# Two pads in on-chip memory that move the weight slots of a two-layer decoder trunk from 288 to 96 bytes past a multiple of 512

## The chip, the core and the metric

The kernel runs on one core of one Trainium2 chip. The metric is the device time of one execution in microseconds (us), and the median of several executions is quoted. Five engines work side by side: TensorE (PE; its weight loads are shown as PEld), VectorE (DVE), ScalarE (ACT), GpSimd (POOL) and SyncE (SP), whose queue issues nearly all transfers. SBUF, the on-chip memory, has 128 partitions; a tile of shape [128, n] in 4-byte numbers takes 4n bytes at the same place in every partition. "Place" below means that byte offset in the partition, modulo 512.

## The reference

It computes two layers of a conditioned decoder trunk for 256 tokens with 1024 features, in 32-bit floats, and a last RMSNorm. Each layer has three sub-layers, whose shift, scale and gate come from `mod = silu(c) @ w_ada[l] + b_ada[l]`:

```python
x = x + 0.5 * g1 * swiglu(modulate(x, sh1, sc1), ffn1_gate, ffn1_up, ffn1_down)
x = x + g2 * token_mix(modulate(x, sh2, sc2), ...)
x = x + 0.5 * g3 * swiglu(modulate(x, sh3, sc3), ffn2_gate, ffn2_up, ffn2_down)
```

`swiglu(u)` is `(silu(u @ w_gate) * (u @ w_up)) @ w_down` with 2816 hidden features. `token_mix` projects `u` with one matrix, runs two attention branches, gates them and multiplies with `w_out`.

## The kernel before

**Exact products from split operands.** A weight is read from memory in pieces of 1 MB into one of four `raw` slots. `split_unit` (lines 147 to 175) cuts a piece into units of 1024 columns: ACT copies a rounded part to `whi` (line 169) and DVE writes the remainder to `wlo` (line 174). Activations are split the same way (`uhi`/`ulo`, `hh`/`hl`, `oa`, `ob`, `yt`, `yk`). Each product is three matmuls, hi by hi, hi by lo and lo by hi. All matmuls are issued by the helper `mm`, so their line is 103; transposes have line 106.

**Two forms of product.** In `ws_tile` the weight part is the stationary operand (128 by 128) and the activations of 256 tokens stream past it: 24 matmuls of 256 columns for a unit. In `xs_group` the activations are stationary and the weight part streams: 12 matmuls of 512 columns for a unit. Names in the trace are out<-moving,stationary: `mm<-uhi,whi` is the first form, `mm<-whi,hh` the second.

**Where the parts of a weight lie.** There are four ordinary slots for a unit, in the pool `wsp` (four `whi`, four `wlo`). During a feed-forward sub-layer the pool `fu` has three more. Units take them in turn, four from `wsp` and then three from `fu`, by `unit_kinds[:] = ["w"] * 4 + ["f"] * EXTRA`, beginning anew with each such sub-layer. The mixer uses `wsp` and, for some units, tiles that are free at the time (`ux`, `uq`, `us` and others). One feed-forward sub-layer has 66 units: 8 of the second form for the first 512 hidden features, 36 of the first form for the other nine groups of gate and up, and 22 of the second form for the down product. The very first sub-layer has 12, 32 and 22, since `begin` makes the first 768 hidden features in another order. A mixer has 8 units of the first form in `wsp` with `uhi`/`ulo` streaming, and 10 units of the second form in `wsp` against `oa`, `ob` and `yt`.

**Places.** The pools are laid out in the order in which the code opens them: `const`, `raws`, `wsp`, `keep`, `scr`, `small`, and then, for one sub-layer at a time, `ffn` with `fu`, or `tm`. The sizes of their tiles give these places modulo 512:

| Tiles | Place before |
|---|---|
| the four `raw` slots | 288 |
| the four ordinary `whi` and `wlo` slots (`wsp`) | 288 |
| `x`, `uhi`, `ulo` and all of `keep` and `scr` | 288 |
| `hh`, `hl`, `oa`, `ob`, `yt`, `ux`, `uq`, `us`, the first sub-layer's `room` (`ffn`, `tm`) | 96 |
| the three further `whi` and `wlo` slots (`fu`) | 96 |
| `yk` (`tm`) | 192 |

A stationary block of a unit of the first form is 512 bytes long, and the next one begins where it ends; `uhi` and `ulo` advance by 1024 bytes; a streaming row of 512 columns is 2048 bytes. So within a unit the place of each operand stays what the table says.

**Order.** SP's queue issues the weights' transfers in order, each when the `raw` slot is released by DVE (or ACT). Splits run in order on ACT and DVE, with the work on adaLN vectors (`ada_half`, line 217) between them. Between sub-layers, `norm_mod` needs the whole residual sum and its square sum, so that PE has little to do for a short time; this is called a handover below. The first sub-layer's `begin` has its own order, with weights landing in the `room` tiles, which lie where `hh` and `hl` will be.

Of the kernel before, what the change touches and what calls it, by code (L numbers as in the profile page):

```python
# [10 lines left out]
F32 = mybir.dt.float32  # L11
# [5 lines left out]
P = 128  # L17
# [17 lines left out]
def shape_tables():  # L35
    f = np.float32
    tab = np.zeros((P, TAB_END), f)
    r = np.arange(P)[:, None]
    k = np.arange(S)[None, :]
    dist = (P + r - k).astype(f)  # L40
    vis = k <= P + r
    tab[:, TAB_D:TAB_D + S] = np.where(vis, dist, f(NEG))
    tab[:, TAB_M:TAB_M + S] = np.where(vis, f(0), f(NEG))
    slopes = np.array(SLOPES, f)
    cend = 16 * np.arange(16) + 31
    c = np.zeros((P, NH, H, 16), f)
    for hf in range(NH):
        t = hf * P + np.arange(P)
        ok = (cend[None, :] <= t[:, None]) & (np.arange(16) < 15)[None, :]
        dd = (t[:, None] - cend[None, :]).astype(f)  # L50
        c[:, hf] = np.where(ok, dd, f(NEG))[:, None, :]
    tab[:, TAB_C:TAB_C + NH * H * 16] = c.reshape(P, -1)
    half = 16
    inv = (10000.0 ** (-np.arange(half, dtype=np.float64) / half)).astype(f)
    ang = (np.arange(S, dtype=f)[:, None] * inv[None, :]).astype(f)
    cos, sin = np.cos(ang.astype(np.float64)).astype(f), np.sin(ang.astype(np.float64)).astype(f)
    sc = f(-(96.0 ** -0.5))
    tt = np.full((P, S), sc, f)
    tt[64:80] = tt[80:96] = cos.T * sc
    tt[96:112] = -sin.T * sc  # L60
    tt[112:128] = sin.T * sc
    tab[:, TAB_T:TAB_T + S] = tt
    cs = np.concatenate([cos, cos], 1).reshape(NH, P, 32).transpose(1, 0, 2)
    sn = np.concatenate([-sin, sin], 1).reshape(NH, P, 32).transpose(1, 0, 2)
    tab[:, TAB_COS:TAB_COS + 64] = cs.reshape(P, 64)
    tab[:, TAB_SIN:TAB_SIN + 64] = sn.reshape(P, 64)
    hh = np.arange(P)[:, None] // 16
    tab[:, TAB_BD:TAB_BD + H] = np.where(hh == np.arange(H)[None, :], f(0.5), f(0))
    tab[:, TAB_SL:TAB_SL + H] = slopes[None, :]
    # slopes are powers of two: queries carry -1 / (8 slope) exactly  # L70
    tab[:64, TAB_Q:TAB_Q + 4] = f(-0.125) / slopes[None, :4]
    tab[64:, TAB_Q:TAB_Q + 4] = f(-0.125) / slopes[None, 4:]
    tab[:, TAB_COL:TAB_COL + 32] = (np.arange(P)[:, None] % 32 == np.arange(32)[None, :]).astype(f)
    return tab
# [3 lines left out]
def hybrid_trunk(ctx, tc, t, out):  # L78
    nc = tc.nc
# [4 lines left out]
    EXTRA = 3            # pairs of weight parts that the feed-forward phases hold beyond four  # L84
    DELAY = (3, 4)       # units of products before a half's operands are turned
    SPLITS_AHEAD = (0, 6)
    keep = ctx.enter_context(tc.tile_pool(name="keep", bufs=1))
# [32 lines left out]
    nc.scalar.activation(cact, c_in, AF.Silu)  # L120
    x = keep.tile([P, NH, D], F32, name="x")
    colmask = tab[:, TAB_COL:TAB_COL + 32]

# [15 lines left out]
    # a normalisation that the tensor engine will wait for is not to queue behind later splits  # L139
# [3 lines left out]
    def hold(n, dve, act):  # L143
        """the splits from the n-th on queue behind these"""
        holds.append([n, dve.ins, act.ins])
# [32 lines left out]
    # shift and scale as columns [feature % 128, feature // 128]; gates as rows on every partition  # L178
    mods = {}

    def column_sums(ps, vec, a, start, stop):
        """ps[32 i + *, j * 32 + r] += sum over partitions of vec * a[:, j * 128 + 32 i + r]"""
        av = a.rearrange("p (j i r) -> p j i r", j=4, i=4)
        for i in range(4):
            mm(ps[32 * i:32 * i + 32, :P].rearrange("p (j r) -> p j r", j=4), vec, av[:, :, i, :], start, stop)
# [118 lines left out]
    def norm_mod(hf, uhi, ulo, sc, sh):  # L304
        """chain on the vector engines now; returns the rest, with its transposes, to be run later"""
        r, a, sq = half_rstd(hf)
        xn = scr.tile([P, D], F32, name="xn", tag="s4")
        for b in range(2):
            i = nc.vector.tensor_scalar(xn[:, b * 512:(b + 1) * 512], x[:, hf, b * 512:(b + 1) * 512], r, a,
                                        ALU.mult, ALU.mult)  # L310
        hold(SPLITS_AHEAD[hf], i, sq)

        def rest(bs=(0, 1)):
            for b in bs:
                uf = scr.tile([P, 4, P], F32, name="uf", tag="uf", bufs=2)
                ps = trps()
                for i in range(4):
                    tr(ps[:, i * P:(i + 1) * P], xn[:, (b * 4 + i) * P:(b * 4 + i + 1) * P])
                for i in range(4):
                    k = b * 4 + i  # L320
                    if i % 2 == 1:
                        nc.scalar.activation(uf[:, i, :], ps[:, i * P:(i + 1) * P], AF.Identity,
                                             scale=sc[:, k:k + 1], bias=sh[:, k:k + 1])
                    else:
                        nc.vector.tensor_scalar(uf[:, i, :], ps[:, i * P:(i + 1) * P],
                                                sc[:, k:k + 1], sh[:, k:k + 1], ALU.mult, ALU.add)
                o = slice(hf * P, (hf + 1) * P)
                nc.scalar.activation(uhi[:, b * 4:b * 4 + 4, o], uf, AF.Copy)
                nc.vector.tensor_tensor(ulo[:, b * 4:b * 4 + 4, o], uf,  # L329
                                        uhi[:, b * 4:b * 4 + 4, o].bitcast(F32), ALU.subtract)  # L330
        return rest

    # work put off by some units of a product
# [25 lines left out]
    def xs_gemm(units, shi, slo, n, evac, tail, post=None):  # L359
        """out[token half, n] = u^T.T @ W; units: (split on demand, [k...]); the last `tail` units  # L360
        are run for the first half of the tokens, then for the second"""
        xs_group([(units, n, evac, tail)], shi, slo, post)

    def xs_group(gemms, shi, slo, post=None):
        """products with the same stationary operand; all their tails by token half"""
# [34 lines left out]
    def stream_units(wv, nk, n, kper, uper, ada_every=0, kinds=None):  # L400
        """wv: [P, nk, n] DRAM view; raw pieces of kper k-tiles, units of uper."""
# [34 lines left out]
    def ffn(l, which, uhi, ulo, ada_plan, post, xn=None, side=None):  # L436
# [4 lines left out]
        with tc.tile_pool(name="ffn", bufs=1) as fp, tc.tile_pool(name="fu", bufs=EXTRA) as fu, \  # L441
# [10 lines left out]
            # the first four tiles token-major, so that they can begin with half of the tokens  # L452
            gp = []

            def finish_rows(hf, gate, up, f0):
                """the product of both for some tiles, token-major, turned"""
# [20 lines left out]
            def begin():  # L477
                """the first sub-layer's start: its shift and scale come in quarters of the features, each
                followed by these features' products with six tiles of hidden features"""
# [6 lines left out]
                # weights wait where the hidden features will be  # L486
# [141 lines left out]
    def token_mix(l, uhi, ulo, ada_plan, post):  # L628
        uhk, ulk = ktiles(uhi), ktiles(ulo)
        w_in = t["w_in"][l].rearrange("(k p) n -> p k n", p=P)  # L630
        with tc.tile_pool(name="tm", bufs=1) as tp, tc.tile_pool(name="aps", bufs=2, space=PSUM) as aps:
# [7 lines left out]
            # merge gates, token-major: tanh(g/2)  # L639
# [20 lines left out]
            # nsa gates, compressed q and kv of the latent branch, rotary key: token-major  # L660
# [21 lines left out]
            # rstd of cq (scaled sums) and ckv together  # L682
# [4 lines left out]
            # compressed branch: windows of k, v  # L687
# [19 lines left out]
            # selected and window keys, feature-major, split, each key head on both halves of the partitions  # L707
# [41 lines left out]
            # gelu (tanh form), doubled; keys on partitions 0-63, values on 64-127  # L749
# [11 lines left out]
            # values, token-major [tok, khalf, (s, w), (g, dv)]  # L761
# [38 lines left out]
            # values, token-major  # L800
# [10 lines left out]
            # rotary key, twice, on partitions 64-127  # L811
# [21 lines left out]
            def latent_operands(j):  # L833
                """queries and keys of heads 2j, 2j+1 with the rotary parts on partitions 64-127"""
# [30 lines left out]
            # q, feature-major, both parts of a head stacked: with the doubled keys two products are exact  # L865
# [22 lines left out]
            # compressed scores, softmax  # L888
# [35 lines left out]
            def softmax(s, pv, dist, slope, gcol):  # L924
                """s[:, a] <- gate * softmax(-slope * (pv[:, a] + dist)); dist is huge where masked"""
# [259 lines left out]
```

## Time and profile before

| | |
|---|---|
| median of 3 runs | 1209.77 us (1209.32 to 1212.08) |
| profiled execution, first to last instruction | 1209.5 us |
[...]
| PE matmul busy | 1172.7 us, 97% |
| DVE busy | 946.5 us, 78% |
| ACT busy | 641.2 us, 53% |
| 16 DMA engines, queue of the weights | 68.9% of the span |

Busy time of PE is modelled and overlapping, so that the interval from the start of one matmul to the start of the next is a better measure of its pace than the duration of one. The profiled execution's span lies 0.3 us under the median of the runs.

### The profile page before, as it was taken

What the parts mean: (1) busy time and instruction counts of PE and PEld (TensorE: products, weight loads), DVE (VectorE), ACT (ScalarE), POOL (GpSimd) and SP (SyncE); (2) the same over time, 40 slices, a digit from 0 to 9 for tenths busy, and PEclk for the clock granted to TensorE, in tenths of its full rate; (3) what the DMA queues carried; (4) which work ended last, traced back from release to release, by engine and by line L of the source; (5) the groups of instructions that cost most, each with busy time, mean ns of one, the idle gap of its engine ahead of it and who ended that gap; (6) DMA issues with size and microseconds to landing.
All of it is one profiled execution on the core that took longest, in us unless ns stands there. A gap on an engine that the chain in (4) does not pass through costs nothing.

```text
span 1209.5 us, 20210 instructions
## 1 busy us (share of the span) xinstructions
PE 1172.7 (97%) x7886; PEld 1027.3 (85%) x7886; DVE 946.5 (78%) x1885; ACT 641.2 (53%) x1152; POOL 19.1 (2%) x17
## 2 busy tenths in 40 slices
PE   5999999899999999999999999999999999999997
PEld 3799987689867889998879999787997778999985
DVE  4998997878888898798478879955878888865553
ACT  4444544547676564434465445444677756554441
POOL 0000000100000000000000000001000000000000
PEclk9999999999999999999999999998999999999999
DMA  9989999495623578898739989954664254885530
GB/s 328 336 294 321 344 336 337 152 253 174 174 102 108 174 229 287 286 311 311 248 110 312 311 274 360 340 168 137 178 188 115 83 187 128 288 263 197 174 140 35
DMA packets 201970, 274.95 MB, mean 227 GB/s; under 512 B 13613, under 2 KB 119815, under 8 KB 201875
## 3 DMA queue, kind: packets, MB, share of 16 engines
q1 hardware_dynamic: 201119, 273.02, 68.9%
q8 instruction: 62, 1.02, 0.3%
q10 hardware_dynamic: 756, 0.64, 0.2%
q14 instruction: 33, 0.27, 0.1%
HBM read 272.60 MB, written 1.05 MB: 226 GB/s over the span
## 4 chain that ended last, share of the span: by engine, by line
PE 86%; DVE 7%; DMA 3%; issue 2%; ACT 1%; SPq 1%; DVEq 0%; ACTq 0%
PE mm L103 77%; PE tr L106 3%; DVE wlo L174 2%; DMA raw<-in_w_ada 2%; PE sc L103 2%; PE po L103 2%; PE tr L103 2%; ACT whi L169 0%; DVE rs L297 0%; DVE acc L217 0%; DVE x L432 0%; DVE rtmp L431 0%; DMA c_in<-in_c 0%; DVE win L702 0%; DVE acc L520 0%
## 5 line engine op out<-in xcount | busy, mean ns | idle before, releaser
L174 DVE TENSOR_TENSOR wlo<-raw,whi 128x1024 fp32r<-128x1024 f32 (+5 forms) x400 | 427.8, 1084 | 128.4 <-ACT whi L169 127.2
L169 ACT ACTIVATE whi<-raw 128x1024 fp32r<-128x1024 f32 (+5 forms) x400 | 364.1, 936 | 236.9 <-PE mm L103 103.9
L103 PE MATMUL mm<-uhi,whi 128*128 128x256 f32 x1248 | 353.1, 283 | 0.0
L103 PE MATMUL mm<-ulo,whi 128*128 128x256 f32 x1248 | 351.8, 282 | 0.0
L103 PE MATMUL mm<-uhi,wlo 128*128 128x256 f32 x1248 | 351.8, 282 | 0.0
L103 PEld LDWEIGHTS mm<-uhi,whi 128*128 128x128 f32 x1248 | 238.9, 191 | 2.4 <-issue 1.4
L103 PEld LDWEIGHTS mm<-ulo,whi 128*128 128x128 f32 x1248 | 237.5, 190 | 0.5
L103 PEld LDWEIGHTS mm<-uhi,wlo 128*128 128x128 f32 x1248 | 237.4, 190 | 0.0
L217 DVE SCALAR_TENSOR_TENSOR acc<-raw,cact,acc 128x512 f32<-128x512 f32 x224 | 166.9, 747 | 6.0 <-DMA raw<-in_w_ada 3.1
L103 PE MATMUL mm<-whi,hh 128*128 128x512 f32 x352 | 139.5, 396 | 0.0
L103 PE MATMUL mm<-wlo,hh 128*128 128x512 f32 x352 | 138.2, 393 | 0.0
L103 PE MATMUL mm<-whi,hl 128*128 128x512 f32 x352 | 138.2, 393 | 0.0
L103 PE MATMUL mm<-whi,uhi 128*128 128x512 f32 (+3 forms) x336 | 126.9, 380 | 3.9 <-ACT uhi L533 2.6
L103 PE MATMUL mm<-wlo,uhi 128*128 128x512 f32 (+3 forms) x336 | 125.9, 375 | 3.7 <-DVE wlo L174 3.7
L103 PE MATMUL mm<-whi,ulo 128*128 128x512 f32 (+3 forms) x336 | 127.2, 379 | 1.7 <-DVE ulo L329 1.7
L103 PEld LDWEIGHTS mm<-whi,hh 128*128 128x128 f32 x352 | 66.0, 187 | 16.5 <-issue 1.6
L103 PEld LDWEIGHTS mm<-whi,hl 128*128 128x128 f32 x352 | 66.0, 188 | 15.4
L103 PEld LDWEIGHTS mm<-wlo,hh 128*128 128x128 f32 x352 | 66.0, 188 | 14.7
L474 ACT ACTIVATE hh<-hf 128x256 fp32r<-128x256 f32 x70 | 29.2, 417 | 92.1 <-DVE hf L473 91.9
L103 PEld LDWEIGHTS mm<-whi,uhi 128*128 128x128 f32 x336 | 63.5, 190 | 14.8 <-ACT uhi L533 3.4
L103 PEld LDWEIGHTS mm<-wlo,uhi 128*128 128x128 f32 x336 | 64.0, 190 | 14.0 <-DVE wlo L174 4.8
L103 PEld LDWEIGHTS mm<-whi,ulo 128*128 128x128 f32 x336 | 64.0, 191 | 12.5 <-DVE ulo L329 3.5
(241 smaller groups left out, 1344.3 us busy)
## 6 DMA issues: line engine op xcount, KB each, us to landing
raw<-in_w_ada SPq DMA_DIRECT2D x72, 1024.0 KB, 8.8
raw<-in_ffn_gate SPq DMA_DIRECT2D x41, 1024.0 KB, 6.6
raw<-in_ffn_up SPq DMA_DIRECT2D x41, 1024.0 KB, 6.0
raw<-in_ffn_down SPq DMA_DIRECT2D x40, 1024.0 KB, 7.5
raw<-in_w_in SPq DMA_DIRECT2D x18, 1024.0 KB, 5.5
raw<-in_w_in SPq DMA_DIRECT2D x16, 512.0 KB, 6.4
raw<-in_w_out SPq DMA_DIRECT2D x8, 1024.0 KB, 5.3
raw<-in_ffn_down SPq DMA_DIRECT2D x8, 512.0 KB
```

Source lines behind the costliest of these rows:

```text
L103: nc.tensor.matmul(o, a, b, start=start, stop=stop)
L106: nc.tensor.transpose(o, a, ident)
L169: nc.scalar.activation(a, s, AF.Copy)
L174: nc.vector.tensor_tensor(b, s, a.bitcast(F32), ALU.subtract)
L217: nc.vector.scalar_tensor_tensor(acc, rv[:, jj, :], cj, binit if j + jj == 0 else acc, ALU.mult, ALU.add)
L474: nc.scalar.activation(h[0][:, f, :], hf32, AF.Copy)
```

## The change

The new code takes two tiles that nothing reads: 320 bytes in `const`, and 192 bytes in `keep` ahead of `x`. POOL clears each once near the start.

```diff
     cact = const.tile([P, KD], F32, name="cact")
     nc.scalar.activation(cact, c_in, AF.Silu)
+    apart = keep.tile([P, 48], F32, name="apart")
+    nc.gpsimd.memset(apart, 0.0)
     x = keep.tile([P, NH, D], F32, name="x")
     colmask = tab[:, TAB_COL:TAB_COL + 32]

+    def pad(pool, nbytes):
+
+        p = pool.tile([P, nbytes // 4], F32, name="pad", tag="pad%d" % nbytes, bufs=1)
+        nc.gpsimd.memset(p, 0.0)
+    pad(const, 320)
```

The rest of the diff removes comments. By the order of the pools the 320 bytes move `raws` and `wsp` from place 288 to place 96 (288 + 320 = 512 + 96). The 192 bytes make it 512 bytes in all for everything from `x` on, which therefore keeps its place modulo 512: `uhi`, `ulo` stay at 288, `hh`, `hl` and the slots of `fu` at 96. The four `raw` slots move along with the ordinary weight slots, and two small constant tiles that come after the pad (`bcols`, `cols`) move as well.

## Rows read from the trace of the kernel before

**Rows 1.** The page: PE busy; DMA share by 40 slices; the chain by engine.

```profile
PE 1172.7 (97%) x7886; PEld 1027.3 (85%) x7886; DVE 946.5 (78%) x1885; ACT 641.2 (53%) x1152; POOL 19.1 (2%) x17
...
DMA  9989999495623578898739989954664254885530
...
PE 86%; DVE 7%; DMA 3%; issue 2%; ACT 1%; SPq 1%; DVEq 0%; ACTq 0%
```

**Rows 2.** Timeline of PE, 1094 to 1115 us, at unit starts: start us, duration us.

```profile
1094.77 0.28 PE L103 MATMUL mm<-uhi,whi 128*128 128x256 f32 x1
...
1097.65 0.28 PE L103 MATMUL mm<-uhi,whi 128*128 128x256 f32 x1
...
1106.29 0.28 PE L103 MATMUL mm<-uhi,whi 128*128 128x256 f32 x1
...
1109.12 0.28 PE L103 MATMUL mm<-uhi,whi 128*128 128x256 f32 x1
...
1114.77 0.28 PE L103 MATMUL mm<-uhi,whi 128*128 128x256 f32 x1
```

**Rows 3.** Timeline of PE in a down product, 1154 to 1174 us.

```profile
1154.31 0.39 PE L103 MATMUL mm<-whi,hh 128*128 128x512 f32 x1
...
1165.51 0.39 PE L103 MATMUL mm<-whi,hh 128*128 128x512 f32 x1
...
1173.69 0.39 PE L103 MATMUL mm<-whi,hh 128*128 128x512 f32 x1
```

**Rows 4.** Timeline of PE from the first mixer's end into the next sub-layer.

```profile
405.66 1.55 PE L103 MATMUL mm<-ux,yt 128*128 128x512 f32 x6
...
408.42 2.97 PE L103 MATMUL mm<-us,yk 128*128 128x512 f32 x12
411.23 0.40 PE L103 MATMUL mm<-whi,yt 128*128 128x512 f32 x1
...
414.02 0.39 PE L103 MATMUL mm<-whi,yk 128*128 128x512 f32 x1
...
423.33 0.39 PE L103 MATMUL mm<-whi,uhi 128*128 128x512 f32 x1
...
428.80 0.40 PE L103 MATMUL mm<-whi,uhi 128*128 128x512 f32 x1
...
431.09 0.39 PE L103 MATMUL mm<-whi,uhi 128*128 128x512 f32 x1
...
433.83 0.39 PE L103 MATMUL mm<-whi,uhi 128*128 128x512 f32 x1
```

**Rows 5.** Groups by form: DVE's remainder of a unit, by source: busy us, mean ns.

```profile
L174 DVE TENSOR_TENSOR wlo<-raw,whi 128x1024 fp32r<-128x1024 f32 x320 | 391.9, 1234 | 112.4 <-ACT whi L169 111.7
...
L174 DVE TENSOR_TENSOR wlo<-room,whi 128x1024 fp32r<-128x1024 f32 x8 | 9.6, 1220 | 3.7 <-ACT whi L169 3.7
```

**Rows 6.** Waits: who waited for whom, us in total, times, longest us.

```profile
ACT whi L169 <- PE mm L103: 105.9, 94, 3.3
...
PE mm L103 <- DVE wlo L174: 3.7, 2, 1.9
```

**Rows 7.** DMA, 11.5 to 13.5 us, then 44.5 to 46.5 us.

```profile
DMA packets 425, 0.76 MB, mean 378 GB/s; under 512 B 27, under 2 KB 85, under 8 KB 425
...
DMA packets 409, 0.74 MB, mean 368 GB/s; under 512 B 22, under 2 KB 77, under 8 KB 409
```

**Rows 8.** The chain at the handovers after both `ffn1`: start us, us.

```profile
213.45 0.70 DVE rtmp L431
...
234.22 1.84 PE mm L103 x8
...
803.21 0.70 DVE rtmp L431
...
824.83 17.18 PE mm L103 x72
```

**Rows 9.** Windows in the second of them: PE, PEld, DVE, ACT, POOL busy, granted clock, DMA.

```profile
821.00:824.00 3.00, 2.25 (x9) 1.47 (x8) 2.62 (x7) 2.60 (x4) 0.33 (x1) 0.50 0.96 322
824.00:827.00 3.00, 3.00 (x11) 2.52 (x10) 2.73 (x6) 2.30 (x5) 0.00 (x0) 0.59 0.44 134
```

## Prediction

> **What bounds the kernel now.** I read the page first. PE is busy for 97% of the span, and the chain that ended last runs through PE for 86% of it, with DVE at 7% and DMA at 3% [rows 1]. A change of PE's pace is therefore worth its full amount unless the feed of weights cannot follow. The waits say that it mostly can: PE's matmuls waited for a split only twice, 3.7 us in total, while ACT waited 105.9 us for PE to give a weight slot back [rows 6]. In other words, over much of the run the splits are ahead of PE and stand still until PE has used a slot.
>
> The second view is the timeline of PE inside the feed-forward products, and it carries the argument. The change alters no instruction there, only places; so I looked for a place that already shows a different pace. The kernel makes that comparison itself, because its units take four slots at place 288 and then three slots at place 96 in turn, with the same instructions on the same streaming operand.
>
> **Gate and up (first form, 24 matmuls of 256 columns per unit).** From 1094.77 to 1106.29 us lie four units from the ordinary slots, 11.52 us, so 2.880 us each; from there to 1114.77 us lie three units from the further slots, 8.48 us, so 2.827 us each [rows 2]. The streaming operand is at 288 throughout. So a unit costs 0.053 us more, 2.2 ns per matmul, when the weights that are loaded behind it lie at 288 too than when they lie at 96. Inside a unit the weights advance by 512 bytes and the streaming operand by 1024 and the pace does not change, so higher bits of the address can't be what matters; that leaves the place modulo 512, or something about the pools themselves (a rival, below). After the change the ordinary slots are at 96, and I take 2.827 us for them. By the rule of four and three, 21 of the 36 units are ordinary in three sub-layers, and 18 of 32 in the first: 81 units x 0.053 = 4.3 us.
>
> **Down (second form, 12 matmuls of 512 columns per unit).** Here the weight streams and `hh` and `hl`, at 96, are stationary. Four ordinary units take 1165.51 - 1154.31 = 11.20 us, 2.800 each; three further ones take 1173.69 - 1165.51 = 8.18 us, 2.727 each [rows 3]. The difference is 0.073 us, 6 ns per matmul. 13 of the 22 units are ordinary in each of four sub-layers: 52 x 0.073 = 3.8 us.
>
> **The mixers.** Eight units per layer have the first form with `uhi` and `ulo`: 16 x 0.053 = 0.85 us. Ten per layer stream from ordinary slots against operands at 96 (`oa`, `ob`, `yt`). Near 411 us 12 such matmuls take 414.02 - 411.23 = 2.79 us, and 12 that stream from tiles at 96 against the same `yt` take 408.42 - 405.66 = 2.76 us [rows 4]; this is a gain of 0.03, against 0.073 in the down product. Between these ends I take 0.05, since the sample here is short and the down product has the same two places: 20 x 0.05 = 1.0 us, between 0.6 and 1.5. In the mixers PE is not always what ends last; I count three quarters, 1.4 us of 1.85.
>
> **Products that I cost at nothing.** The second form against `uhi`/`ulo`, at 288: 24 matmuls from ordinary slots take 428.80 - 423.33 = 5.47 us, 0.228 us each, and 12 from the further slots 433.83 - 431.09 = 2.74 us, again 0.228 [rows 4]. Place 96 brings nothing there. Against `yk`, at 192, streaming from 96 takes 411.23 - 408.42 = 2.81 us for 12; only two units per layer are touched, so even 0.02 us for each is under 0.1 us. The 192 matmuls of the mixers that stream `cT` (already at 96) past ordinary weights go from a pair (96, 288) to a pair (96, 96), of which I have no undisturbed row; at 2.2 ns either way that is 0.4 us up or down, and I take zero.
>
> **The other things that move.** The splits read a `raw` slot at 288 and write an ordinary slot at 288; both go to 96. DVE's remainder took 1220 ns on average when its source was `room`, at 96, and 1234 ns from `raw` [rows 5], so I see no cost and count no gain. POOL clears two small tiles once; POOL is busy 2% [rows 1], its clears come after the one that the start needs, and nothing reads the result. Cost nothing; were the start to wait for them, it would be a fraction of a microsecond. The landings in `raw` are a rival, below.
>
> [...] In the rows the pace of a matmul depends on where the weights lie that are loaded behind it: 2.880 against 2.827 us per unit [rows 2]. [...]
>
> **Sum.** 4.3 + 3.8 + 1.4 = 9.5 us. The profiled span of 1209.5 us becomes 1200.0 us; the median of the runs is 0.3 us above the profiled span, so the forecast is 1200.3 us, 0.8% less.
>
> **Rivals.**
>
> *A, place is not the cause.* The further slots are also in another pool and far away, and the gain may belong to that. [...] For it: the further slots differ from the ordinary ones in more than place. Against it: the ordinary and the further slots keep the same pace against `uhi` [rows 4], so the further pool is not faster in general; and the down product, where a streaming operand gains, while in gate and up it is the stationary one. Chance 7%.
>
> *B, the feed takes part of it.* In the first `ffn1` the DMA share is at nine tenths or more in most slices from 60 to 210 us [rows 1], so its splits may be only as early as memory lets them. If that sub-layer gains nothing (18 x 0.053 + 13 x 0.073 = 1.9 us) and the mixers neither (1.4 us), the gain is 9.5 - 3.3 = 6.2 us and the time 1203.6 us. Against it: PE's two waits for a split [rows 6] are short, so there is a reserve for PE to run into. Chance 11%.
>
> *C, landing at 96 is slower, and the kernel ends above 1209.8 us.* All weights land in the `raw` slots, which move. Twelve of the 40 slices, 363 us, have a DMA share of nine tenths or more [rows 1]. Were a transfer longer by a fraction f, these stretches would be longer by up to 363 f: at 2.6% that eats the 9.5 us, at 3.3% the kernel is slower by 0.2%, at 4% it ends at 1214.8 us. In the first sub-layer some weights land in `room`, at 96, and later ones of the same shape in `raw`, at 288: by the order of issue these fill two windows of 2 us, with 378 GB/s at 96 and 368 GB/s at 288 [rows 7]. That speaks against any penalty of a per cent or more. [...] Chance 5%.
>
> *The clock.* [...] This is no case of its own; it widens the range by 1.7 us on either side.
>
> **How the numbers follow.** Forecast 77%, B 11%, A 7%, C 5%. The forecast's own bounds: at best 4.3 + 3.8 + 0.85 + 1.5 + 0.4 = 10.9 us, and one spell fewer, gives 1197.2 us, which I round to 1196.8 us for the reading of times to 0.01 us; at worst B plus one spell gives 1205.3 us. I give 1196.8 to 1205.3 us, which leaves out A, C and a rest of the others, about 2 in 10. A difference of 0.2%, 2.4 us, is about what a measurement of this kernel can tell from no change. Faster by more than that: the forecast and most of B, 0.88. Within: A, 0.07. Slower: C, 0.05.
>
> **What would show it.** In the profile of the changed kernel all units of gate and up should start 2.83 us apart without the rhythm of four and three, and all units of a down product 2.73 us apart; second-form units against `uhi` should stay at 0.228 us a matmul. DVE's remainder should stay at 1.22 us and the DMA rate in the first 200 us the same. The prediction is wrong if the ordinary slots keep 2.88 us (A), if the pace is 2.83 us but PE waits for `wlo` in the first layer (B), or if the DMA slices lengthen (C).

## The result and the profile after

| | before | after |
|---|---|---|
| median of 6 runs each | 1211.38 us | 1195.36 us |
| lowest and highest | 1209.32 to 1212.08 us | 1193.99 to 1203.15 us |
| span of the profiled execution | 1209.5 us | 1193.5 us |
| mean granted TensorE clock in it | 0.995 | 0.994 |

The ratio is 0.9887, with a 95% interval of 0.9866 to 0.9907. The kernel is 16.0 us faster; the forecast was 9.5 us. The direction and the place of the gain were right, and the time lies 1.4 us under the lower end of the range.

The page of the changed kernel answers to [rows 1]: busy time, DMA share by 40 slices, chain by engine.

```profile
PE 1156.5 (97%) x7886; PEld 1016.1 (85%) x7886; DVE 946.5 (79%) x1885; ACT 640.8 (54%) x1152; POOL 19.4 (2%) x19
...
DMA  9989999586623579989739979954664253985540
...
PE 87%; DVE 7%; DMA 2%; issue 2%; ACT 1%; SPq 1%; DVEq 0%; ACTq 0%
```

PE has the same 7886 matmuls and 16.2 us less busy time. DVE and ACT work as long as before, and the chain still runs through PE. So PE does the same work at a quicker pace.

The timeline of PE at unit starts, in the gate and up products of the last sub-layer, answers to [rows 2]. At 1080.39 us four ordinary units begin, at 1091.70 three further ones, and at 1100.18 ordinary ones again.

```profile
1080.39 0.28 PE L103 MATMUL mm<-uhi,whi 128*128 128x256 f32 x1
...
1091.70 0.28 PE L103 MATMUL mm<-uhi,whi 128*128 128x256 f32 x1
...
1100.18 0.28 PE L103 MATMUL mm<-uhi,whi 128*128 128x256 f32 x1
```

Four ordinary units now take 11.31 us, 2.828 each, and three further ones 8.48 us, 2.827 each. This is exactly what was forecast: the rhythm of four and three is gone. Another sub-layer of the same execution shows something that was not forecast. Its timeline begins with the eight short matmuls of a column sum.

```profile
524.45 0.43 PE L103 MATMUL tr<-acc,ones 128*32 128x128 f32 x8
...
527.64 0.28 PE L103 MATMUL mm<-uhi,whi 128*128 128x256 f32 x1
...
533.09 0.28 PE L103 MATMUL mm<-uhi,whi 128*128 128x256 f32 x1
...
541.25 0.28 PE L103 MATMUL mm<-uhi,whi 128*128 128x256 f32 x1
```

From 527.64 to 533.09 us lie two ordinary units (2.725 each) and from there to 541.25 us three further ones (2.720). The same instructions with operands at the same places have two paces: 2.72 us for 24 matmuls is 113.3 ns each, and 2.827 us is 117.8 ns.

The quick pace was there before the change too, in stretches that the prediction had not looked at. This is the timeline of the kernel before:

```profile
517.58 0.42 PE L103 MATMUL tr<-acc,ones 128*32 128x128 f32 x8
...
520.78 0.28 PE L103 MATMUL mm<-uhi,whi 128*128 128x256 f32 x1
...
526.22 0.28 PE L103 MATMUL mm<-uhi,whi 128*128 128x256 f32 x1
```

These two further units take 5.44 us, 2.72 each, where further units behind ordinary ones take 2.827 [rows 2].

The down product answers to [rows 3] (four ordinary units, three further ones) and the second form against `uhi` to [rows 4]; both are timelines of the changed kernel.

```profile
420.82 0.39 PE L103 MATMUL mm<-whi,uhi 128*128 128x512 f32 x1
...
426.32 0.39 PE L103 MATMUL mm<-whi,uhi 128*128 128x512 f32 x1
...
1136.52 0.39 PE L103 MATMUL mm<-whi,hh 128*128 128x512 f32 x1
...
1147.40 0.39 PE L103 MATMUL mm<-whi,hh 128*128 128x512 f32 x1
...
1155.56 0.39 PE L103 MATMUL mm<-whi,hh 128*128 128x512 f32 x1
```

All units of the down product take 2.72 us (10.88 / 4 and 8.16 / 3). The 24 matmuls against `uhi` take 5.50 us, 0.229 us each, as before.

DVE's remainder by source, in the groups by form (busy us, mean ns; answers to [rows 5]):

```profile
L182 DVE TENSOR_TENSOR wlo<-raw,whi 128x1024 fp32r<-128x1024 f32 x320 | 392.0, 1235 | 106.7 <-ACT whi L177 105.9
...
L182 DVE TENSOR_TENSOR wlo<-room,whi 128x1024 fp32r<-128x1024 f32 x8 | 9.7, 1221 | 3.5 <-ACT whi L177 3.5
```

The waits (us, times, longest; answer to [rows 6]):

```profile
ACT whi L177 <- PE mm L103: 102.3, 91, 3.3
...
PE mm L103 <- DVE wlo L182: 3.7, 2, 1.9
```

The splits take as long as they did, ACT still waits some 100 us for PE to give slots back, and PE waits no more for splits than before. The faster PE met no new wait.

The granted clock by windows (PE, PEld, DVE, ACT, POOL busy, clock, DMA share, GB/s), beside [rows 9]:

```profile
30.00:34.00 4.00, 4.00 (x14) 3.23 (x13) 3.77 (x10) 1.01 (x3) 0.00 (x0) 0.57 1.08 366
...
228.00:231.00 3.00, 2.31 (x6) 1.30 (x4) 2.63 (x6) 1.36 (x3) 1.58 (x1) 0.50 0.82 251
```

This execution had the half clock near the start and at the first handover; the profiled one of before had it at the second handover only. It matters for the table below, where the timelines of both executions are cut at the same places of the program.

| Stretch (where it ends before and after, us) | before | after | change |
|---|---|---|---|
| start to ordinary units (69.21, 70.77) | 69.21 | 70.77 | +1.56 |
| gate and up 1, to its down product (158.00, 156.87) | 88.79 | 86.10 | -2.69 |
| down 1, mixer 1, handovers (449.14, 446.44) | 291.14 | 289.57 | -1.57 |
| gate and up 2 (552.61, 546.78) | 103.47 | 100.34 | -3.13 |
| down 2, handover (643.61, 636.88) | 91.00 | 90.10 | -0.90 |
| gate and up 3 (747.79, 737.89) | 104.18 | 101.01 | -3.17 |
| down 3, mixer 2, handovers (1038.48, 1025.37) | 290.69 | 287.48 | -3.21 |
| gate and up 4 (1140.53, 1125.62) | 102.05 | 100.25 | -1.80 |
| down 4 to the end (1209.5, 1193.5) | 68.97 | 67.88 | -1.09 |

Gate and up gain 10.8 us, where 4.3 us were forecast. The loss at the start goes with the half clock: in a second profile of the changed kernel (e10 below), where the clock from 30 to 34 us was 1.00, the ordinary units begin at 69.17 us.

### The profile page after: what moved, and what is told of

It reads as the page before. It is cut to its first block, busy times and chain, and to the rows that moved or that the text cites. A ratio compares the mean times of both kernels' runs of the same rounds, so it can differ in the third digit from the quotient of the medians.

```text
span 1193.5 us, 20212 instructions
## 1 busy us (share of the span) xinstructions
PE 1156.5 (97%) x7886; PEld 1016.1 (85%) x7886; DVE 946.5 (79%) x1885; ACT 640.8 (54%) x1152; POOL 19.4 (2%) x19
## 4 chain that ended last, share of the span: by engine, by line
PE 87%; DVE 7%; DMA 2%; issue 2%; ACT 1%; SPq 1%; DVEq 0%; ACTq 0%
PE mm L103 78%; PE tr L106 3%; DVE wlo L182 3%; PE sc L103 2%; PE po L103 2%; DMA raw<-in_w_ada 2%; PE tr L103 2%; DVE win L710 1%; ACT whi L177 0%; DVE rs L305 0%; DVE rtmp L439 0%; DVE x L440 0%; DMA c_in<-in_c 0%; DVE kd L732 0%; DVE acc L528 0%
## 5 line engine op out<-in xcount | busy, mean ns | idle before, releaser
L103 PE MATMUL mm<-uhi,whi 128*128 128x256 f32 x1248 | 348.7, 279 | 0.0
L103 PE MATMUL mm<-uhi,wlo 128*128 128x256 f32 x1248 | 347.3, 278 | 0.0
L103 PE MATMUL mm<-ulo,whi 128*128 128x256 f32 x1248 | 347.3, 278 | 0.0
L103 PEld LDWEIGHTS mm<-uhi,whi 128*128 128x128 f32 x1248 | 234.3, 188 | 2.5 <-issue 1.8
L103 PEld LDWEIGHTS mm<-uhi,wlo 128*128 128x128 f32 x1248 | 234.4, 188 | 0.0
```

The source lines that it names most:

```text
L103: nc.tensor.matmul(o, a, b, start=start, stop=stop)
```

## The experiments

Each kernel below lays its tiles out with the same two pads in other sizes or pools, unless said otherwise. "Ordinary" and "further" are the slots of `wsp` and `fu`. All ratios are to the kernel before, run on the same chip in the same rounds.

**e1, the streams moved in place of the weights.** `x`, `uhi`, `ulo` and the rest of `keep` go to 96; everything else keeps its place, the ordinary slots and `raw` at 288.

```diff
-    apart = keep.tile([P, 48], F32, name="apart")
+    apart = keep.tile([P, 80], F32, name="apart")
-    pad(const, 320)
+    pad(scr, 192)
```

> Ordinary weight slots and raw slots stay at 288; x, uhi, ulo and the rest of keep go to 96; everything after keeps its place. Theory 'own place' (weights that lie at 96 are fast, whatever streams): gate and up units keep the rhythm of before, 2.88 us for the four ordinary slots and 2.83 us or less for the three further ones, and the time stays within 2 us of before. Theory 'pair' (a 256-column product is slow only when the stream and the weights loaded behind it lie at the same place): the rhythm turns round, ordinary slots 2.83 us or less, further slots (now the same place as uhi) 2.88 us; time about 1 us under before, within 3 us. Down products are unchanged in both, 2.80 and 2.73 us per unit.

Measured: 1206.79 us (1205.72 to 1207.48), ratio 0.9956, 0.9941 to 0.9971. Timeline, four ordinary units from 1092.21 and three further ones from 1103.09 us:

```profile
1092.21 0.28 PE L103 MATMUL mm<-uhi,whi 128*128 128x256 f32 x1
...
1103.09 0.28 PE L103 MATMUL mm<-uhi,whi 128*128 128x256 f32 x1
...
1111.73 0.28 PE L103 MATMUL mm<-uhi,whi 128*128 128x256 f32 x1
```

The rhythm is turned round: the ordinary slots, untouched at 288, take 2.72 us, and the further ones, untouched at 96, take 2.88 us. So neither the pool nor a slot's own place is slow in the first form, but the pair: a stream and weights at the same place. In the second form 288 remains the slower place for a streaming weight (2.80 against 2.73 us in the down product), and against `uhi`, now at 96, it went from 229.8 to 233.2 ns a matmul in the feed-forward sub-layers. The time fell by 5.4 us, where about 1 us had been expected, because the ordinary units had gained up to 0.16 us each and the further ones had lost 0.05.

The quick and the slow pace both occur in e1 as well, in the ordinary slots, but behind other starts. This is its timeline behind a column sum:

```profile
504.17 0.43 PE L103 MATMUL tr<-acc,ones 128*32 128x128 f32 x8
...
507.46 0.28 PE L103 MATMUL mm<-uhi,whi 128*128 128x256 f32 x1
...
513.11 0.28 PE L103 MATMUL mm<-uhi,whi 128*128 128x256 f32 x1
```

Two ordinary units take 5.65 us, 2.825 each, and so it is behind all six column sums that stand ahead of ordinary units in e1. Right behind further units, which have the same place as the stream there, 14 of 17 blocks of ordinary units are quick. In the kernel before it is the other way round: the 17 blocks that come right behind same-place units are all slow (2.827 us), and the three that come behind a column sum are quick. Modulo 256 the ordinary weights of e1 lie 64 bytes below the stream (32 against 96), those of the changed kernel 64 bytes above it (96 against 32); whether that makes the difference was not tested.

**e2, only the `raw` slots moved; e3, only the weight slots.**

```diff
 e2
-    apart = keep.tile([P, 48], F32, name="apart")
-    nc.gpsimd.memset(apart, 0.0)
     pad(const, 320)
+    pad(wsp, 192)
 e3
-    pad(const, 320)
+    pad(wsp, 320)
```

> Only the raw slots, in which the transfers land, go to 96; the ordinary weight slots stay at 288 and all else keeps its place. If the weight slots are the cause of the gain: no change, ratio 0.998 to 1.002, units 2.88 and 2.83 us. If the landing place bears part of the gain: the part of the 16 us that goes beyond the predicted 9.5 us shows here, ratio near 0.995. If landing at 96 is dearer: ratio above 1.002 and longer DMA slices.

> Only the ordinary weight slots go to 96; the raw slots stay at 288. If the weight slots are the whole cause: the full gain, ratio 0.985 to 0.991 as with both moved, with gate and up units at 2.72 and 2.83 us in long stretches. If the raw slots bear a part: ratio near 0.993.

Measured: e2 1212.24 us (1208.27 to 1213.11), ratio 0.9994, 0.9981 to 1.0006; e3 1194.69 us (1192.51 to 1199.48), ratio 0.9863, 0.9839 to 0.9886. Timeline of e2 (four ordinary units, three further):

```profile
1095.79 0.28 PE L103 MATMUL mm<-uhi,whi 128*128 128x256 f32 x1
...
1107.31 0.28 PE L103 MATMUL mm<-uhi,whi 128*128 128x256 f32 x1
...
1115.79 0.28 PE L103 MATMUL mm<-uhi,whi 128*128 128x256 f32 x1
```

Its DMA from 44.5 to 46.5 us:

```profile
DMA packets 419, 0.73 MB, mean 367 GB/s; under 512 B 28, under 2 KB 93, under 8 KB 419
```

With `raw` at 96 the units keep 2.88 and 2.827 us, and the landings keep their rate (367 GB/s against 368, [rows 7]). In e3 long stretches of units run at 2.72 us (from 447.46 us) and at 2.827 us (from 466.98 us), as expected. The whole gain belongs to the weight slots.

**e4, a stream started anew.** The changed kernel, with one more column sum that nothing reads, issued once in the last sub-layer where its units run at 2.83 us. The helper is also that of e9.

```diff
+    def nudge():
+        column_sums(trps(), ones[:, :32].bitcast(F32), tab[:, :512], True, True)
...
+                if (l, which, grp) == (1, 2, 4):
+                    nudge()
```

> The changed kernel, plus a short group of eight 32-column matmuls whose result nothing reads, once in the last feed-forward sub-layer, ahead of its fifth group of hidden features; the same group (the adaLN column sums) stands ahead of stretches at 2.72 us in the changed kernel. Theory 'latch' (with weights at 96 and the stream at 288 a product has two paces, and the start of the stream decides which one holds until it is interrupted): units from there to the down product take 2.72 us in place of 2.83 us, some 23 units x 0.107 = 2.5 us, less 0.5 us for the group: about 2 us under the changed kernel. Rival 'surroundings' (the pace follows what DVE, ACT and the transfers do at the time): units stay at 2.83 us and the time is 0.4 us longer.

Measured: 1194.42 us (1193.45 to 1197.14), ratio 0.9859, 0.9844 to 0.9873. Timeline behind the group of eight:

```profile
1045.33 0.43 PE L103 MATMUL tr<-tab,ones 128*32 128x128 f32 x8
...
1048.51 0.28 PE L103 MATMUL mm<-uhi,whi 128*128 128x256 f32 x1
...
1053.95 0.28 PE L103 MATMUL mm<-uhi,whi 128*128 128x256 f32 x1
...
1056.68 0.63 PE L103 MATMUL tr<-acc,ones 128*128 128x512 f32 x2
...
1059.97 0.28 PE L103 MATMUL mm<-uhi,whi 128*128 128x256 f32 x1
...
1065.62 0.28 PE L103 MATMUL mm<-uhi,whi 128*128 128x256 f32 x1
```

Behind the eight short matmuls two units take 5.44 us, 2.72 each. Behind the two matmuls of 512 columns that make a gate row, at 1056.68 us, two units take 5.65 us, 2.825 each, and so it goes on to the end. The pace does follow the start of the stream. The gain in time did not come: the expectation had overlooked that the next gate row comes four units later, and four units by 0.107 us, less the group itself, can't be measured.

**e5 to e8, other places for the ordinary slots** (320, 352, 416 and 32; `raw` goes along, all else stays). The diff is that of e5; for the two numbers e6 has 112 and 64, e7 96 and 128, e8 64 and 256.

```diff
-    apart = keep.tile([P, 48], F32, name="apart")
+    apart = keep.tile([P, 120], F32, name="apart")
-    pad(const, 320)
+    pad(const, 32)
```

> Pads as in the change but of 32 and 480 bytes: ordinary weight and raw slots at 320, all else at its place. Theory 'exact pair' (256-column products are slow only when stream and weights have the very same place): gate and up units at 2.72 or 2.83 us as at 96. Theory 'distance' (near places collide in part, far ones do not): 32 bytes off uhi stays near 2.88 us. Down units, where hh and hl lie at 96: 2.73 us if 288 is a bad place by itself, 2.80 us if every place but that of hh is slow.

> Slots at 352, 64 bytes past uhi. Exact pair: gate and up units 2.72 or 2.83 us. Distance: between 2.83 and 2.88 us. Down: 2.80 us if every place but that of hh is slow, otherwise 2.73 us.

> Slots at 416, 128 bytes past uhi. Exact pair and distance alike: gate and up units 2.72 or 2.83 us; a period of 128 bytes in the collisions would show as 2.88 us. Down: 2.80 us if every place but that of hh is slow, otherwise 2.73 us.

> Slots at 32, 256 bytes from uhi at 288 and 64 bytes from hh at 96. Exact pair and distance alike: gate and up units 2.72 or 2.83 us; a period of 256 bytes would show as 2.88 us. Down: 2.80 us if every place but that of hh is slow, otherwise 2.73 us.

Timelines in the order e5, e6, e7, e8. In each kernel the first two rows enclose four ordinary units, and the second and third three further ones:

```profile
1087.70 0.28 PE L103 MATMUL mm<-uhi,whi 128*128 128x256 f32 x1
...
1099.06 0.28 PE L103 MATMUL mm<-uhi,whi 128*128 128x256 f32 x1
...
1107.22 0.28 PE L103 MATMUL mm<-uhi,whi 128*128 128x256 f32 x1
```

```profile
1101.71 0.28 PE L103 MATMUL mm<-uhi,whi 128*128 128x256 f32 x1
...
1113.02 0.28 PE L103 MATMUL mm<-uhi,whi 128*128 128x256 f32 x1
...
1121.50 0.28 PE L103 MATMUL mm<-uhi,whi 128*128 128x256 f32 x1
```

```profile
1089.47 0.28 PE L103 MATMUL mm<-uhi,whi 128*128 128x256 f32 x1
...
1100.85 0.28 PE L103 MATMUL mm<-uhi,whi 128*128 128x256 f32 x1
...
1109.02 0.28 PE L103 MATMUL mm<-uhi,whi 128*128 128x256 f32 x1
```

```profile
1095.85 0.28 PE L103 MATMUL mm<-uhi,whi 128*128 128x256 f32 x1
...
1107.37 0.28 PE L103 MATMUL mm<-uhi,whi 128*128 128x256 f32 x1
...
1115.85 0.28 PE L103 MATMUL mm<-uhi,whi 128*128 128x256 f32 x1
```

| Ordinary slots at | time, us | ratio (95%) | ordinary unit, first form | further unit | down unit from ordinary slots |
|---|---|---|---|---|---|
| 320 (e5) | 1204.37 | 0.9941 (0.9918 to 0.9964) | 2.84 us | 2.72 | 2.80 |
| 352 (e6, two runs) | 1196.42 | 0.9864 (0.9830 to 0.9898) | 2.828, elsewhere 2.72 | 2.827, elsewhere 2.72 | 2.72 |
| 416 (e7) | 1204.40 | 0.9924 (0.9892 to 0.9955) | 2.845 | 2.72 | 2.75 |
| 32 (e8) | 1210.76 | 0.9991 (0.9976 to 1.0006) | 2.88 | 2.827 | 2.80 |

32 behaves as 288 and 352 as 96, both 256 apart. In these two pairs it is the place modulo 256 that counts, not modulo 512, as the table of places gives it. 320 and 416 each have a pace of their own, between that of the same place and the good one. No theory of these expectations had that: by the exact pair and by the distance 416 was to give 2.72 or 2.83 us, and by the exact pair 320 too; by the distance 320 was to stay near 2.88 us. In the down product 352 is as good as 96 and 416 lies between, so that neither "288 is bad by itself" nor "every place but that of `hh`" holds as it was put. In e5 and e7 the ordinary units are still slow, but most of the further units between them take 2.72 us (mean of the intervals 114.0 and 114.1 ns). So not every slow unit sets the next ones back; in the kernel before and in e8 those at the same place modulo 256 do, in e1 mostly not.

**e9, the column sum behind the last gate row; e10, the change beside it.** e9 is the changed kernel with the helper of e4 in three sub-layers.

```diff
+                if xn is None and grp == 5:
+                    nudge()
```

> The change, with eight further matmuls of 32 columns (a column sum that nothing reads, some 0.45 us with its wait) behind the sixth group of gate and up, once in each of three feed-forward sub-layers, all three after the sub-layer's last group of two 512-column adaLN matmuls. Theory (a stream of first-form products keeps the pace with which it starts, and the eight short matmuls make it start at the quick one): from the group on, units that follow it start 2.72 us apart where the changed kernel has 2.83; in the last sub-layer, which runs at 2.83 to its end, that is about 20 units by 0.108 = 2.2 us less 0.45; in the two others the stream is already quick for part of the rest, so 0 to 0.9 us each, less 0.45: a gain of 1.5 to 2.5 us over the changed kernel, ratio 0.998 to 0.999 of it. Rival (the pace belongs to the sub-layer and its surroundings, not to how the stream starts): units stay 2.83 us apart and the three groups cost 1.3 us, ratio 1.001.

> The changed kernel itself, beside the run with the three column sums. Both theories: about 0.988 of the kernel before, the units of the last sub-layer 2.83 us apart to its end.

Measured: e9 1195.14 us (1191.28 to 1197.64), ratio 0.9869, 0.9845 to 0.9894; e10 1195.50 us (1193.67 to 1196.97), ratio 0.9879, 0.9860 to 0.9898. Timeline of e9 in the last sub-layer:

```profile
1055.30 0.63 PE L103 MATMUL tr<-acc,ones 128*128 128x512 f32 x2
1055.86 0.43 PE L103 MATMUL tr<-tab,ones 128*32 128x128 f32 x8
...
1059.04 0.28 PE L103 MATMUL mm<-uhi,whi 128*128 128x256 f32 x1
...
1118.88 0.28 PE L103 MATMUL mm<-uhi,whi 128*128 128x256 f32 x1
```

and of e10 in the same place:

```profile
1055.69 0.62 PE L103 MATMUL tr<-acc,ones 128*128 128x512 f32 x2
...
1058.97 0.28 PE L103 MATMUL mm<-uhi,whi 128*128 128x256 f32 x1
...
1118.33 0.28 PE L103 MATMUL mm<-uhi,whi 128*128 128x256 f32 x1
```

In e9 22 units take 59.84 us, 2.72 each; in e10 21 units take 59.36 us, 2.827 each. The pace with which the stream starts is kept for more than 500 matmuls, and the rival (the surroundings) falls. From the gate row to the down product e9 needs 66.30 us against 68.30, 2.0 us less, where 2.2 less 0.45 was expected. Of the two other sub-layers the later one gains 0.26 us. The earlier one was 0.30 us ahead at 536.06 us, but its stream turned slow there, and at the down product nothing of that was left. The spans of the two profiled executions differ by 2.4 us (1189.5 and 1191.9). The medians differ by only 0.36 us, and the intervals of the two ratios overlap almost wholly, so that a gain in time over the change is not shown.

## Why the prediction was right in kind and too small

The intervals counted here lie between neighbouring matmuls of the same product and are shorter than 135 ns with 256 columns and 250 ns with 512, so that waits are left out.

**Second form: right.** The down product was put at 0.073 us for each ordinary unit and gave 0.08 in the stretch shown. Over all 604 intervals from the start of one such matmul to the start of the next, the mean fell from 233.3 to 227.2 ns: 3.7 us against the 3.8 forecast. Against `uhi` nothing changed (229.7 and 229.8 ns), as forecast. Against `oa`, `ob` and `yt` the mean of 192 intervals went from 233.3 to 228.6 ns, 0.9 us, where 1.0 us had been forecast.

**First form: the pair was right, its price was not.** The step that failed is "After the change the ordinary slots are at 96, and I take 2.827 us for them", with nothing counted for the further slots. 2.827 us is not the pace of place 96; it is the pace of further units that begin behind ordinary ones. The rows that stood behind it [rows 2] had been chosen in one sub-layer, where every further unit is slow. The change takes the same-place units away, and with them what sets the stream back in this kernel (e1 shows that it need not be so with other places). The ordinary units then take 2.72 or 2.83 us, and the further ones gain as well. Over all 2298 intervals with ordinary slots the mean fell from 119.9 to 115.2 ns, 10.7 us; over 1400 with further slots from 117.0 to 115.5 ns, 2.2 us. This makes 12.9 us, where 4.3 us and three quarters of 0.85 us had been forecast.

**`cT`: a loss where nothing was taken.** These products got both operands at 96. Over 172 and 175 intervals the mean rose from 116.4 to 119.6 ns, 0.55 us lost; the bound was 0.4 us either way. It is the same-place price, as in gate and up (119.9 ns before).

**The sum.** 12.9 + 3.7 + 0.9 - 0.55, and 0.35 for the further slots of the down product (422 intervals, 0.8 ns each), is 17.3 us of PE's time; 16.0 us came out. The 1.3 us between them is what other engines or the clock may have taken; the start alone, with its half clock, lost 1.56 us. How much of the mixers' part lay on the path was not tested by itself. The prediction's lower end of 1196.8 us is also 0.4 us under the 1197.2 us that its own terms give; the gain went past both.

**The rivals.** A, by which the time was to stay at that of before, falls by e1, where the pools keep their places and change their paces: in the stretches shown the ordinary slots go from 2.88 to 2.72 us, the further ones from 2.827 to 2.88. In e1 and e8 alike the pace goes with the places of both operands: 2.88 us per unit at the same place modulo 256, 2.72 or 2.83 at 64 bytes' distance. B did not show: PE's two waits for a split stayed at 3.7 us, and the first gate and up gained 2.69 us. C falls by e2, 0.9994: for landings at 96 in place of 288 no price is seen in it, with 367 GB/s against 368 in the window from 44.5 us. The clock was forecast as a spread, and the profiled executions showed it: leaving out the last microseconds, which the executions before and after spend at half clock (0.50 from 1205.33 and from 1190.55 us), there was one spell at a granted clock of 0.50 before (from 819.6 us), two after (from 30.0 and 228.0 us) and none in e10, whose mean granted clock was 0.998. The 1.7 us that the range counts for one spell is the author's estimate from [rows 8] and [rows 9] (0.85 us by the chains of the two handovers, 0.8 us by the window at 0.59), and no run shows it as a whole; the spell at the start of the changed kernel went with a loss of 1.56 us.

**What stays open.** Why in the first form a distance of 64 bytes is good (2.72 or 2.83 us a unit), 32 and 128 poor (2.84 and 2.845) and 0 worst (2.88), and why the second form against `uhi` does not mind the same place (229.7 ns at 288 and 229.5 at 32), was not tried. Nor is it settled what makes a start quick. In the changed kernel all nine streams behind a column sum of eight matmuls were quick, and seven of eight behind a gate row were slow; one, at 100.75 us, was quick. In e1 the streams behind column sums were slow. The ordinary units from 70.77 us on were slow in one profile of the changed kernel, and quick in the other from 69.17 us. That the changed kernel's times spread more than those of before would fit this, but was not tested.

## What to carry to other kernels

Where a kernel is bound by TensorE and streams one tile past weights that are loaded from another, read the start-to-start intervals by slot and try other places modulo 256 for the two tiles. Here 64 bytes' distance was best with 256 columns (2.72 or 2.83 us a unit, against 2.88 at no distance) and no distance in the down product with 512 (2.72 us, against 2.75 to 2.80 at other distances), so that each product has to be measured; two pads gave 1.1%. Before a pace is taken from a trace as a price, look at the same instruction in several stretches: a value that is steady in one of them can hang on what ran ahead of it. Moving one tile changes each pair that it belongs to, so list the products that become equal as well as those that become different.

## What the runs showed of the hardware

Matmuls of 256 columns with weights loaded behind them started 120 ns apart when both operands lay at the same place modulo 256: both at 288 before, at 32 and 288 in e8, both at 96 in e1. At 64 bytes' distance they had two paces, 113.3 and 117.8 ns; in the last sub-layer of e9 a stream kept the pace with which it started for 22 units, with nothing between. In the two other sub-layers of e9 a quick stream turned slow at an interval of 128 ns, at 536.29 us; another, with an interval of 136 ns at 727.91 us, stayed quick. Matmuls of 512 columns that streamed the weight past `hh` at 96 started 227 ns apart with the weight at 96 or 352, 229 ns at 416, and 233 ns at 32, 288 or 320: there the same place is the quick one.
